# Seven products for the second group's first tile pair, with a raw tile outside the pool, in a two-layer decoder trunk

## The chip, the cores and the metric

The kernel runs on one core of one Trainium2 chip. A core has TensorE (PE in the profile; its weight loads are PEld), VectorE (DVE), ScalarE (ACT), GpSimd (POOL) and SyncE (SP), which here only issues transfers. The metric is the device time of one execution in microseconds, lower is better; the figure shown is the median of several runs.

## The reference, cut to what matters

A trunk of two layers over 512 tokens and 16 meta tokens (L = 528), model width 1024, float32. Each layer is a mixer and an MLP, each followed by a LayerNorm. Both MLPs have the change.

```python
def sq_relu_mlp(h, w1, w2):            # w1: 1024 x 4096, w2: 4096 x 1024
    return jnp.square(jax.nn.relu(h @ w1)) @ w2

for i in range(DEPTH):                 # DEPTH = 2
    mix = retention_gdn_mixer(...) if i % 2 == 0 else mamba2_mixer(...)
    h = layer_norm(DN_ALPHA * h + mix, ln1_w[i], ln1_b[i])
    h = layer_norm(DN_ALPHA * h + sq_relu_mlp(h, mlp_w1[i], mlp_w2[i]), ln2_w[i], ln2_b[i])
return h[:, N_META:]
```

## The kernel before, in words

Activations lie feature-major: a tile has 128 features on the partitions and tokens along the columns. Every float32 operand of a large product is split into a rounded high part and the low rest (`split`, L152 a cast on ScalarE and L153 a subtraction on VectorE), and a product is three matmuls: high by high, high by low, low by high (`mm3`, L172 to L174). Tokens come in two halves: 272 and 256 columns in layer 0, 256 and 256 in layer 1; layer 1 also has the form with 512 columns at once (`both` in `phase`).

**Order.** The Python program writes instructions in an order, with background generators (`tasks`) that `tick()` moves on by a step after each tile. A scheduler at compile time then sets, by its own cost estimates and by that order as priority, the order on each engine; it also waits for buffers. On the chip each engine works through its list in order, and so does SP's queue of transfers.

**Raw weights.** `wtile` takes a tile of 128 x 1024 from the pool "w" of 12. `fetch` (L160) loads a raw tile, `halve` takes two more for its high and low parts, and the raw tile is free when it is split.

**The norm.** `norm_after` spawns a task for each half. It transposes, normalises, transposes back, and for each of 8 tiles m writes the high part on ScalarE (L337), the whole value on VectorE (L339) and the low part `hl` by a subtraction (L340), on VectorE for m = 3 and 7, else on POOL.

**The MLP.** `mlp` goes through the 4096 hidden features in 8 groups of 4 tiles. The first product of a group is either classical, one tile at a time (`phase`), or goes by `Unit`: two tiles at once as a 2 x 2 block product with seven block products of 12 matmuls in place of eight (Winograd's form of Strassen, L510). A unit's `prepare` loads three raw tiles (t1, t2 and x; L472, L473), forms four sums and differences on VectorE (L483 to L487) and splits seven operands; its `run` copies three partial results on ScalarE (L514, L517, L520) and adds them on VectorE (L523, L527, L531). The other factor of the block product are combinations of the norm's output, formed once per MLP by `combos` on VectorE and split (L404, L153), collected in `tt`. Each hidden tile is then passed through ReLU and square (`evac_u`: L447 and L455 on ScalarE, L449 on POOL, L456 on VectorE). `Four` is the second product: four output tiles of one group, accumulated on VectorE (L381 the first time, L379 later).

Before, group 0 is classical: three tiles in the head (first halves of all three, then, when the norm's second half is ready, their second halves), then the fourth. Of group 1, tiles 0 and 2 are classical and 1 and 3 a unit. From there a list of stages runs; during stage i, `adv` moves on the preparation of stage i + 1, and the fetches of stage i + 2 are issued at its start:

```python
        stages = [unit(1, 1), four(0, 0), four(0, 1)]
        for c in range(2, NG):
            stages += [unit(c, 0), four(c - 1, 0), unit(c, 1), four(c - 1, 1)]
```

The last group's second product is done by `Rows` and `final` in layer 1, with the last LayerNorm in it; its weight and bias (`lnf`) lie in the tile that held the tables of layer 0's mixer (`cr`).

Of the kernel before, what the change touches and what calls it, by code (L numbers as in the profile page):

```python
# [57 lines left out]
def trunk(ctx: ExitStack, tc: tile.TileContext, a, out):  # L58
# [7 lines left out]
    def nm(p):  # L66
        count[0] += 1
        return f"{p}{count[0]}"
# [29 lines left out]
    def spawn(gen):  # L98
        tasks.append(gen)
        return gen  # L100
# [18 lines left out]
    def wait(cond):  # L119
        while not cond():  # L120
            yield
# [6 lines left out]
    cst = one("cst", C_COLS)  # L128
    pp = one("pp", PP_COLS)
    rbc = one("rbc", 104)  # L130
    cr = sb.tile([P, R_COLS], F32, tag="cr", bufs=1, name="cr")
    ident = cst[:, C_ID:C_ID + P]
    triu = cst[:, C_TRIU:C_TRIU + P]
    ls = cst[:, C_LS:C_LS + P]
# [19 lines left out]

    def wtile(dt=F32R):
        return sb.tile([P, 1024], dt, tag="w", bufs=12, name=nm("w"))

    def fetch(src, n=1024):
        raw = wtile(F32)
        SY.dma_start(raw[:, :n], src)  # L160
        return raw
# [25 lines left out]
    def phase(tiles, rhs, evac, ns, head=0, tail=0, ready=None):  # L187

        def both(blks, key):
            o = pm(512)
            product(o, blks, rhs[2], every=4)
            for hf in range(2):
                evac(key, hf, o[:, hf * 256:hf * 256 + 256])
            tick()

        def run(hf, blks, key, m=P):
            o = pm(ns[hf], part=m)
            product(o, blks, rhs[hf], m=m)  # L200
            evac(key, hf, o)
            tick()
        n = len(tiles)
        for i0, i1 in [(0, head)] + [(i, i + 1) for i in range(head, n - tail)] + [(n - tail, n)]:
            held = []
            for srcs, *key in tiles[i0:i1]:
                held.append(([b for s in srcs for b in (s if isinstance(s, list) else s() if callable(s) else wload(s))], *key))
                if len(rhs) > 2 and head <= i0 < n - tail:
                    both(*held.pop())
                    continue  # L210
                if ready is not None and i0 == 0:
                    until(lambda: ready(0))
                run(0, *held[-1])
            if ready is not None and i0 == 0:
                until(lambda: ready(1))
            for args in held:
                run(1, *args)
# [91 lines left out]
    def norm_after(r, ns, wcol, bcol):  # L309

        res, pairs = [[], []], []
        if ns[0] + ns[1] == 512:
            res.append([])

        def task(hf):
            n, norm = ns[hf], []

            def apply(off, bn, pt, mean, rstd):
                row = tl("row", 1024)
                t2 = [row[:, j * 512:(j + 1) * 512] for j in range(2)]  # L320
                S.activation(t2[1][:bn], pt[1][:bn, :], AF.Identity, bias=shift(mean, rstd, bn), scale=rstd)
                V.tensor_scalar(t2[0][:bn], pt[0][:bn, :], mean, rstd, op0=SUB, op1=MUL)
                norm.append((off, bn, t2))

            yield from layernorm(r[hf], ns, hf, lambda: hf == 0 or len(res[0]) == KT, apply)
            yield
            for m in range(KT):
                pf = px(n)
                for off, bn, t2 in norm:
                    T.transpose(pf[:, off:off + bn], t2[m // 4][:bn, (m % 4) * P:(m % 4 + 1) * P], ident[:bn, :bn])  # L330
                if hf == 0:
                    pairs.append(htile())
                    if len(res) > 2:
                        res[2] += parts(pairs[m], [(0, 512)])
                hi, lo = parts(pairs[m], [(hf * ns[0], n)])[0]
                w, b = pp[:, wcol + m:wcol + m + 1], pp[:, bcol + m:bcol + m + 1]
                S.activation(hi, pf, AF.Identity, bias=b, scale=w)  # L337
                t = r[hf][m]
                V.tensor_scalar(t, pf, w, b, op0=MUL, op1=ADD)  # L339
                (V if m % 4 == 3 else G).tensor_tensor(lo, t, hi.bitcast(F32), op=SUB)  # L340
                res[hf].append((hi, lo))
        for hf in range(2):
            spawn(task(hf))
        return res, pairs, lambda hf: len(res[hf]) == KT
# [42 lines left out]
    def combos(h, ns, nh, go, get):  # L387

        def quarter(k, c):

            a, b = h[0][k], h[1][k]
            if c == 0:
                return [(0, nh, a[:, 0:nh])]
            cut = ns[0] - nh
            return ([(0, cut, a[:, nh:ns[0]])] if cut else []) + [(cut, nh, b)]

        def diff(out, x, y):
            if not isinstance(y, list):
                y = [(0, nh, y)]
            for o, e, ap in x:  # L400
                for o2, e2, ap2 in y:
                    lo, hi = max(o, o2), min(e, e2)
                    if lo < hi:
                        V.tensor_tensor(out[:, lo:hi], ap[:, lo - o:hi - o], ap2[:, lo - o2:hi - o2], op=SUB)  # L404

        yield from wait(go)
        for k in range(4):
            q0, q1 = [[quarter(i, c) for c in range(2)] for i in (k, k + 4)]
            d = [tl("m", nh) for _ in range(4)]
            diff(d[0], q0[1], q0[0])  # L410
            diff(d[2], q1[1], q0[1])
            diff(d[1], q1[1], d[0])
            diff(d[3], q1[0], d[1])
            for j in range(4):
                get(j, k, d[j])
                if j % 2:
                    yield

    def mlp(l, hx, h, ns, ready, evac0, pairs, final=None):
# [42 lines left out]
        class Unit:  # L462


            def __init__(self, c, i, evac):
                self.src = [w1[l, c * GF + i], w1[l, c * GF + i + 2]]
                self.keys, self.evac, self.ops = (i, i + 2), evac, {}
                self.gen = self.prepare()

            def prepare(self):  # L470
                t1, t2, x = fetch(self.src[0]), wtile(F32), wtile(F32)
                SY.dma_start(x[:, 0:512], self.src[1][:, 0:512])  # L472
                SY.dma_start(t2[:, 512:1024], self.src[1][:, 512:1024])  # L473
                a11, a12, s1, a22, s3, s2 = [y[:, i:i + 512] for y in (t1, t2, x) for i in (0, 512)]
                a21 = s3
                yield

                def sp(x):
                    hi, lo = tl("s", 512, F32R), tl("s", 512, F32R)
                    split(hi, lo, x)  # L480
                    return hi, lo
                s4 = tl("s", 512)
                V.tensor_tensor(s1, a21, a22, op=ADD)  # L483
                V.tensor_tensor(s3, a11, a21, op=SUB)
                yield
                V.tensor_tensor(s2, s1, a11, op=SUB)
                V.tensor_tensor(s4, a12, s2, op=SUB)  # L487
                yield
                self.ops["a11"], self.ops["a12"] = halve(t1)
                yield  # L490
                self.ops["s1"], self.ops["a22"] = halve(t2)
                yield
                self.ops["s2"] = sp(s2)
                yield
                self.ops["s3"] = sp(s3)
                yield
                self.ops["s4"] = sp(s4)
# [88 lines left out]
        def unit(c, i):  # L586
            return Unit(c, i, lambda f, hf, o: groups[c][1](f, hf, o, nh))

        def four(c, i):
            return Four(c, groups[c][0], 4 * i)  # L590

        stages = [unit(1, 1), four(0, 0), four(0, 1)]
        for c in range(2, NG):
            stages += [unit(c, 0), four(c - 1, 0), unit(c, 1), four(c - 1, 1)]
        last = [four(NG - 1, 0), four(NG - 1, 1)] if final is None else [Rows()]
        gens = [st.gen for st in stages + last]
        spawn(combos(h, ns, nh, lambda: ready(1), get))
        phase([([w1[l, f]], f) for f in range(GF)], hx, groups[0][1], ns, head=3, ready=ready)
        spawn(gens[0])
        phase([([w1[l, GF + f]], f) for f in (0, 2)], hx, groups[1][1], ns)  # L600
        until(lambda: "s4" in stages[0].ops and all(x is not None for y in tt for x in y))
        B += [[half(k, 0) for k in range(4)], [half(k, 0) for k in range(4, 8)],
              [half(k, 1) for k in range(4, 8)], tt[3], tt[0], tt[1], tt[2]]
        next(gens[1])
# [389 lines left out]
        put_fm(*done[:3], outs)  # L994
        oF[8 + 2 * hd:10 + 2 * hd] = outs

    dtab, qdec, kdec = cr[:, R_D:R_D + 512], cr[:, R_Q:R_Q + 512], cr[:, R_K:R_K + 8]
    cosT, sinT = cr[:, R_COS:R_COS + L], cr[:, R_SIN:R_SIN + L]

    def rope_tile(block, done):  # L1000
        m1, m2 = tl("s", L), tl("s", L)
# [113 lines left out]
    for hd in range(4):  # L1115
# [1 line left out]
            qF[hd] = f  # L1117
            spawn(gdn_queries(hd))
        conv_tile(a["w0"][4 + hd], gcv[4 + hd], None, done)
    SY.dma_start(cr, a["cstr"])  # L1120
    for hd in range(4):
        got = []
        for i in range(4):
# [35 lines left out]
    h = hn  # L1159


    lnf = sb.tile([P, 2048], F32, tag="cr", bufs=1, name="lnf")
    SY.dma_start(lnf, a["lnf"].unsqueeze(0).to_broadcast([P, 2048]))
    sd = {}

    def ssd_scalars(fm):
# [234 lines left out]
    def final(u, blks, r):  # L1401


        w, b = [lnf[:, j:j + 512] for j in (0, 512)], [lnf[:, j:j + 512] for j in (1024, 1536)]

        def store(t, c0, c1, x, queue=SY):
            queue.dma_start(out[t * P:(t + 1) * P, c0:c1], x)
# [149 lines left out]
```

## Time and profile before

| | |
|---|---|
| time, median of 3 runs | 1700.62 us (1700.37 to 1701.94) |
| time of the profiled execution | 1703.35 us |
| its span, first to last instruction | 1701.6 us |
| granted TensorE clock, mean | 0.991 |
| busy: TensorE, VectorE, ScalarE, POOL | 98%, 68%, 43%, 19% of the span |
| transfers | 155.60 MB, 91 GB/s |

Matmuls overlap each other, so the busy share of TensorE says little; what it really waited for stands in the list of waits, and what a matmul really takes is the distance between two starts. In rows of the order of time, the bracket gives the engine's idle time before the row and what ended it. In the chain of work that ended last, a row is a piece of that chain. In grouped rows stand the count, the busy time in us, the mean in ns, and the idle time before them with what ended it. In rows of stretches of time stand, behind the length, the busy us of PE, PEld, DVE, ACT and POOL with their instructions, then the granted clock of TensorE, the share of the transfer engines and GB/s.

### The profile page before, as it was taken

What the parts mean: (1) busy time and instruction counts of PE and PEld (TensorE: products, weight loads), DVE (VectorE), ACT (ScalarE), POOL (GpSimd) and SP (SyncE); (2) the same over time, 40 slices, a digit from 0 to 9 for tenths busy, and PEclk for the clock granted to TensorE, in tenths of its full rate; (3) what the DMA queues carried; (4) which work ended last, traced back from release to release, by engine and by line L of the source; (5) the groups of instructions that cost most, each with busy time, mean ns of one, the idle gap of its engine ahead of it and who ended that gap; (6) DMA issues with size and microseconds to landing.
All of it is one profiled execution on the core that took longest, in us unless ns stands there. A gap on an engine that the chain in (4) does not pass through costs nothing.

```text
span 1701.6 us, 29956 instructions
## 1 busy us (share of the span) xinstructions
PE 1662.8 (98%) x11884; PEld 1532.8 (90%) x11884; DVE 1152.1 (68%) x2294; ACT 739.7 (43%) x1509; POOL 329.4 (19%) x366
## 2 busy tenths in 40 slices
PE   9999999999999999999999999999999999999998
PEld 7898998899998999999998988888778888888886
DVE  6896666676437766676657776867564686777765
ACT  4432245554214534444434665756432454444441
POOL 1211210010003201111102034232410321111112
PEclk9999999999999999999999999999999999999999
DMA  6233212112221232322221443433222232322321
GB/s 217 81 101 85 72 39 80 45 63 75 87 88 56 94 100 100 100 92 89 94 78 63 127 125 106 118 112 97 84 68 100 74 101 100 100 100 100 100 100 50
DMA packets 88197, 155.60 MB, mean 91 GB/s; under 512 B 11833, under 2 KB 43193, under 8 KB 87801
## 3 DMA queue, kind: packets, MB, share of 16 engines
q1 hardware_dynamic: 87912, 153.53, 28.0%
q8 instruction: 93, 1.52, 0.4%
q14 instruction: 48, 0.39, 0.1%
q10 hardware_dynamic: 144, 0.16, 0.0%
HBM read 148.92 MB, written 4.75 MB: 90 GB/s over the span
## 4 chain that ended last, share of the span: by engine, by line
PE 81%; DVE 7%; DMA 3%; ACT 3%; POOL 3%; issue 2%; SPq 0%; POOLq 0%; DVEq 0%; ACTq 0%
PE pmm L172 18%; PE pmm L174 18%; PE pmm L173 18%; PE pmm L510 8%; PE pmx L510 6%; DVE w L153 1%; PE pmx L1419 1%; DMA w<-in_w 1%; DVE s L633 1%; DMA w<-in_mw 1%; POOL hl L340 1%; PE pmx L1273 1%; DMA row<-rd 1%; PE pmx L1277 1%; PE pmx L270 1%
## 5 line engine op out<-in xcount | busy, mean ns | idle before, releaser
L172 PE MATMUL pmm<-hh,w 128*128 128x256 f32 (+4 forms) x1480 | 456.0, 308 | 4.5 <-ACT s L626 2.6
L173 PE MATMUL pmm<-hl,w 128*128 128x256 f32 (+3 forms) x1480 | 442.3, 299 | 5.5 <-POOL hl L340 4.8
L174 PE MATMUL pmm<-hh,w 128*128 128x256 f32 (+3 forms) x1480 | 443.8, 300 | 0.2 <-DVE w L153 0.2
L152 ACT CAST w<-w 128x1024 fp32r<-128x1024 f32 (+2 forms) x253 | 261.1, 1032 | 410.9 <-PE pmm L174 170.4
L153 DVE TENSOR_TENSOR w<-w,w 128x1024 fp32r<-128x1024 f32 (+2 forms) x253 | 321.3, 1271 | 121.4 <-PE pmm L173 71.5
L172 PE MATMUL pmm<-s,w 128*128 128x256 f32 (+2 forms) x1136 | 361.5, 318 | 0.1
L174 PE MATMUL pmm<-s,w 128*128 128x256 f32 (+2 forms) x1136 | 360.9, 318 | 0.0
L173 PE MATMUL pmm<-s,w 128*128 128x256 f32 (+2 forms) x1136 | 360.4, 317 | 0.0
L172 PEld LDWEIGHTS pmm<-hh,w 128*128 128x128 f32 (+2 forms) x1480 | 279.7, 189 | 18.6 <-issue 4.5
L173 PEld LDWEIGHTS pmm<-hl,w 128*128 128x128 f32 (+1 forms) x1480 | 279.4, 189 | 17.4 <-POOL hl L340 6.1
L174 PEld LDWEIGHTS pmm<-hh,w 128*128 128x128 f32 (+1 forms) x1480 | 279.3, 189 | 8.8 <-DVE w L153 0.7
L174 PEld LDWEIGHTS pmm<-s,w 128*128 128x128 f32 x1136 | 213.8, 188 | 14.6
L172 PEld LDWEIGHTS pmm<-s,w 128*128 128x128 f32 x1136 | 213.9, 188 | 14.4 <-DVE m L381 0.3
L173 PEld LDWEIGHTS pmm<-s,w 128*128 128x128 f32 x1136 | 213.6, 188 | 14.5 <-DVE s L1352 0.3
L449 POOL TENSOR_TENSOR m<-m 128x256 f32<-128x256 f32 (+2 forms) x128 | 120.4, 943 | 512.0 <-ACT m L447 490.2
L147 POOL TENSOR_TENSOR n<-n,neg 128x1 f32<-128x1 f32 (+2 forms) x58 | 40.3, 698 | 440.3 <-DVE n L146 419.7
L633 DVE SCALAR_TENSOR_TENSOR s<-s,pp,s 128x528 f32<-128x528 f32 x120 | 101.7, 848 | 28.1 <-ACT s L631 25.9
L379 DVE TENSOR_TENSOR m<-m,pmm 128x272 f32<-128x272 f32 (+1 forms) x208 | 82.6, 416 | 19.5 <-PE pmm L174 18.8
L456 DVE TENSOR_TENSOR s<-m,s 128x256 fp32r<-128x256 f32 (+2 forms) x128 | 68.2, 535 | 28.5 <-POOL m L449 26.1
L510 PE MATMUL pmm<-s,s 128*128 128x264 f32 (+1 forms) x624 | 85.0, 286 | 2.1 <-ACT row L514 1.8
L510 PEld LDWEIGHTS pmm<-s,s 128*128 128x128 f32 x624 | 79.5, 191 | 2.7 <-ACT row L514 2.0
L1229 POOL TENSOR_TENSOR row<-row,m 128x1024 f32<-128x1024 f32 x16 | 41.0, 2564 | 112.4 <-ACT s L631 57.5
(313 smaller groups left out, 2436.4 us busy)
## 6 DMA issues: line engine op xcount, KB each, us to landing
w<-in_w SPq DMA_DIRECT2D x88, 512.0 KB, 3.3
w<-in_mw SPq DMA_DIRECT2D x172, 256.0 KB, 3.2
w<-in_mw SPq DMA_DIRECT2D x38, 512.0 KB, 3.2
w<-in_wo SPq DMA_DIRECT2D x29, 512.0 KB, 3.5
row<-rd SPq DMA_DIRECT2D x16, 512.0 KB, 5.6
s<-rd SPq DMA_DIRECT2D x32, 128.0 KB, 5.7
w<-in_w2n SPq DMA_DIRECT2D x4, 512.0 KB, 5.6
out<-row SPq DMA_DIRECT2D x7, 256.0 KB, 2.0
```

Of the source, the lines that this page charges most:

```text
L147: G.tensor_tensor(dst, t, neg5[0:part, 0:n], op=POW)
L152: S.copy(dst_hi, src)
L153: V.tensor_tensor(dst_lo, src, dst_hi.bitcast(F32), op=SUB)
L172: T.matmul(o, w[0], x[0], start=first, stop=False)
L173: T.matmul(o, w[0], x[1], start=False, stop=False)
L174: T.matmul(o, w[1], x[0], start=False, stop=last)
L379: V.tensor_tensor(t, t, o, op=ADD)
L449: G.tensor_tensor(q, t, t, op=MUL)
L456: V.tensor_tensor(lo, q, hi.bitcast(F32), op=SUB)
L510: T.matmul(o, w[x][:, c], B[b][k][y], start=first and k == i == 0, stop=last and k == 3 and i == 2, skip_group_check=True)
L633: V.scalar_tensor_tensor(acc, cin[:, k:k + L], w[k], acc, op0=MUL, op1=ADD)
L1229: G.tensor_tensor(g3(rw, 8), g3(rw, 8), bm(cb, 8), op=MUL)
```

## The change

In words: (1) the third raw tile x of a unit no longer comes from the pool of 12 but from one of two tiles, "cra" for a group's first unit and "crb" for its second; these hold layer 0's tables until its mixer is done, loaded by two transfers, and the final norm's weight and bias at the end, now loaded within `final`. (2) In the second half of a norm, VectorE takes the low parts of tiles 3, 5, 6, 7 and POOL those of 0, 1, 2, 4. (3) The raw tile of group 0's fourth tile is fetched behind that of the third, and the fetches of four(0,0) start two ticks after the norm is ready. (4) Group 1's classical pair is gone: unit(1,0) takes its place, and the stages begin with four(0,0), unit(1,0), four(0,1), unit(1,1). (5) `combos` begins one tick later.

```diff
-    cr = sb.tile([P, R_COLS], F32, tag="cr", bufs=1, name="cr")
+    cra, crb = one("cra", R_COS), one("crb", 2 * L)
...
+    def spare(tag):
+
+        return sb.tile([P, 1024], F32, tag=tag, bufs=1, name=nm("sp"))
...
-                (V if m % 4 == 3 else G).tensor_tensor(lo, t, hi.bitcast(F32), op=SUB)
+                (V if m % 4 == 3 or hf == 1 and m > 4 else G).tensor_tensor(lo, t, hi.bitcast(F32), op=SUB)
...
         yield from wait(go)
+        yield
         for k in range(4):
...
-                self.keys, self.evac, self.ops = (i, i + 2), evac, {}
+                self.keys, self.evac, self.ops, self.tag = (i, i + 2), evac, {}, "cr" + "ab"[i]
...
-                t1, t2, x = fetch(self.src[0]), wtile(F32), wtile(F32)
+                t1, t2, x = fetch(self.src[0]), wtile(F32), spare(self.tag)
...
-        stages = [unit(1, 1), four(0, 0), four(0, 1)]
+        def begin():
+            yield from wait(lambda: ready(1))
+            yield from pause(2)
+            yield from gens[0]
+
+        stages = [four(0, 0), unit(1, 0), four(0, 1), unit(1, 1)]
...
         spawn(combos(h, ns, nh, lambda: ready(1), get))
-        phase([([w1[l, f]], f) for f in range(GF)], hx, groups[0][1], ns, head=3, ready=ready)
-        spawn(gens[0])
-        phase([([w1[l, GF + f]], f) for f in (0, 2)], hx, groups[1][1], ns)
-        until(lambda: "s4" in stages[0].ops and all(x is not None for y in tt for x in y))
+        spawn(begin())
+        ahead = []
+
+        def third():
+            blks = wload(w1[l, 2])
+            ahead.append(fetch(w1[l, 3]))
+            return blks
+
+        phase([([w1[l, 0]], 0), ([w1[l, 1]], 1), ([third], 2), ([lambda: halve(ahead[0])], 3)], hx, groups[0][1], ns,
+              head=3, ready=ready)
+
+        until(lambda: len(stages[0].blks) == 4 and all(x is not None for y in tt for x in y))
...
-    dtab, qdec, kdec = cr[:, R_D:R_D + 512], cr[:, R_Q:R_Q + 512], cr[:, R_K:R_K + 8]
-    cosT, sinT = cr[:, R_COS:R_COS + L], cr[:, R_SIN:R_SIN + L]
+    dtab, qdec, kdec = cra[:, R_D:R_D + 512], cra[:, R_Q:R_Q + 512], cra[:, R_K:R_K + 8]
+    cosT, sinT = crb[:, 0:L], crb[:, L:2 * L]
...
-    SY.dma_start(cr, a["cstr"])
+    SY.dma_start(cra, a["cstr"][:, 0:R_COS])
+    SY.dma_start(crb, a["cstr"][:, R_COS:R_COLS])
...
-    lnf = sb.tile([P, 2048], F32, tag="cr", bufs=1, name="lnf")
-    SY.dma_start(lnf, a["lnf"].unsqueeze(0).to_broadcast([P, 2048]))
...
-        w, b = [lnf[:, j:j + 512] for j in (0, 512)], [lnf[:, j:j + 512] for j in (1024, 1536)]
+        w, b = [], []
+        for i, (dst, tag) in enumerate(((w, "cra"), (b, "crb"))):
+            x = spare(tag)
+            SY.dma_start(x, a["lnf"][i * 1024:(i + 1) * 1024].unsqueeze(0).to_broadcast([P, 1024]))
+            dst += [x[:, 0:512], x[:, 512:1024]]
```

## The prediction

> **What bounds the kernel now.** I read the page first, then who waited for whom, then the order of time around the start of each MLP, then the grouped instructions of VectorE (DVE) there.
>
> ```profile
> span 1701.6 us, 29956 instructions
> PE 1662.8 (98%) x11884; PEld 1532.8 (90%) x11884; DVE 1152.1 (68%) x2294; ACT 739.7 (43%) x1509; POOL 329.4 (19%) x366
> PE 81%; DVE 7%; DMA 3%; ACT 3%; POOL 3%; issue 2%; SPq 0%; POOLq 0%; DVEq 0%; ACTq 0%
> ```
>
> TensorE is the bound: 81% of the chain. So time can be won in two ways only: fewer matmuls, or less waiting between them. The rows below are matmuls in order of time (start, duration, line, and in brackets the idle time and its releaser), at the start of MLP 0 and then of MLP 1.
>
> ```profile
> 545.78 0.28 PE L172 MATMUL pmm<-hh,w 128*128 128x256 f32 x1
> 550.87 0.58 PE L173 MATMUL pmm<-hl,w 128*128 128x256 f32 x1 [2.39 <-POOL hl L340]
> 551.24 0.42 PE L174 MATMUL pmm<-hh,w 128*128 128x256 f32 x1
> 551.46 0.42 PE L172 MATMUL pmm<-hh,w 128*128 128x256 f32 x1
> 558.71 0.29 PE L172 MATMUL pmm<-hh,w 128*128 128x272 f32 x1
> 564.58 0.29 PE L172 MATMUL pmm<-hh,w 128*128 128x272 f32 x1
> 576.33 0.28 PE L510 MATMUL pmm<-hh,w 128*128 128x264 f32 x1
> 581.22 2.83 PE L510 MATMUL pmm<-s,s 128*128 128x264 f32 x12 [1.80 <-ACT row L514]
> 590.17 0.28 PE L172 MATMUL pmm<-s,w 128*128 128x272 f32 x1
> ...
> 1351.41 0.29 PE L172 MATMUL pmm<-hh,w 128*128 128x256 f32 x1
> 1356.48 0.58 PE L173 MATMUL pmm<-hl,w 128*128 128x256 f32 x1 [2.38 <-POOL hl L340]
> 1364.29 0.40 PE L172 MATMUL pmm<-hh,w 128*128 128x512 f32 x1
> 1380.94 0.28 PE L510 MATMUL pmm<-hh,w 128*128 128x256 f32 x1
> 1391.80 0.40 PE L172 MATMUL pmm<-s,w 128*128 128x512 f32 x1
> ```
>
> Next, the undisturbed price of a stage, from the chain (start, duration, twelve matmuls of one product): in MLP 0 the first and last product of one unit, the first of the next and the first of the last unit; then first and last product of a unit of MLP 1.
>
> ```profile
> 614.14 1.46 PE pmm L510 x12
> 622.92 1.46 PE pmm L510 x12
> 636.09 1.45 PE pmm L510 x12
> ...
> 857.34 1.46 PE pmm L510 x12
> 1435.42 1.43 PE pmm L510 x12
> 1443.97 1.43 PE pmm L510 x12
> ```
>
> A unit takes 622.92 + 1.46 - 614.14 = 10.24 us in MLP 0, a Four 636.09 - 624.38 = 11.71; in MLP 1 a unit takes 1443.97 + 1.43 - 1435.42 = 9.98. A matmul of 256 columns costs 1.43/12 = 0.119.
>
> With these prices the losses stand out. The second halves of the first three tiles are 72 matmuls of 256 columns, 8.6 us; they take 558.71 - 545.78 = 12.9 and 1364.29 - 1351.41 = 12.9. So 4.3 us go in each MLP: 2.4 of waiting for POOL, and the rest because the matmuls behind it start 0.22 apart (551.24, 551.46), half rate. The first unit takes 590.17 - 576.33 = 13.84 instead of 10.24 (3.6 lost) and 1391.80 - 1380.94 = 10.86 instead of 9.98 (0.9 lost).
>
> **The change part by part.**
>
> *Norm shares.* In the second half the subtractions of tiles 5 and 6 go from POOL to DVE. POOL's last one in MLP 0, and DVE's rows of this stage:
>
> ```profile
> 547.76 3.06 POOL L340 TENSOR_TENSOR hl<-m,hh 128x256 fp32r<-128x256 f32 x1
> 543.46 2.35 DVE L339 TENSOR_SCALAR m<-pmx,pp 128x256 f32<-128x256 f32 x5
> 546.42 1.44 DVE L339 TENSOR_SCALAR m<-pmx,pp 128x256 f32<-128x256 f32 x3
> L340 DVE TENSOR_TENSOR hl<-m,hh x4: 411/672/812, 530.3 to 548.1; 128x272 fp32r<-128x272 f32 x2, 128x256 fp32r<-128x256 f32 x2
> ```
>
> The op that held TensorE is POOL's sixth, 3.06 us to 550.82. Its fifth ended where the sixth begins, at 547.76, so without the last two POOL is done before that. DVE's L339 end at 547.8; three subtractions at 0.41, each starting about 0.08 before its predecessor is done, give tiles 5, 6, 7 at 548.15, 548.5, 548.85. TensorE asks for them at 545.78 + 16 x 0.119 = 547.7, then 0.36 apart. So some 0.5 us of waiting is left, now on DVE, and the gain is 4.3 - 0.5 = 3.8 per MLP, 7.6 in all. Layer 0's last norm gets the same edit; no wait of its matmuls on POOL's hl stands in the list of waits there, so I cost it at nothing; if DVE is late there, it is tenths.
>
> *The pair becomes a unit.* Two classical tiles of group 1: 576.33 - 564.58 = 11.75 in MLP 0; in MLP 1 two of the three tiles in 1380.94 - 1364.29, 11.1. A unit: 10.24 and 9.98. Gain 1.5 + 1.1 = 2.6.
>
> *The order and the fetches.* four(0,0) now stands where the pair stood, so the first unit still has one stage of 11 to 12 us in front of it. Its loss of 3.6 came from late weights:
>
> ```profile
> SPq L549 <- PE pmm L174: 11.8, 1, 11.8
> 579.85 1.04 ACT L152 CAST w<-w 128x1024 fp32r<-128x1024 f32 x1 [1.04 <-DMA w<-in_mw]
> 552.54 0.38 SPq L160 DMA_DIRECT2D w<-in_mw  x1
> 574.55 3.19 SPq L549 DMA_DIRECT2D w<-in_mw  x6
> ```
>
> SP issues in order; after 552.54 it came to a Four's loads and stood 11.8 us until a tile of the pool of 12 was free, so that most of them went out at 574.55. The cast at 579.85 waited for it on ScalarE, with the copy L514 that TensorE needed queued behind. After the change the unit's third raw tile is outside the pool: a Four's four halves, the next unit's two raws and four halves and the next Four's two raws make exactly 12, where they made 13. The third fetch is one issue earlier, the Four's four loads start two ticks after the norm, and nothing waits in SP ahead of them. I take both losses as gone: 3.6 + 0.9 = 4.5.
>
> *Steady stretch.* From 614.14 to 857.34 are 11 steps of a unit and a Four: 243.2 against 11 x 21.95 = 241.4, 1.8 lost; DVE's first sum of a unit (L483) waits for the raw tiles, 27 us in 11 times:
>
> ```profile
> DVE w L483 <- DMA w<-in_mw: 27.0, 11, 3.8
> ```
>
> I take 1.5 of the 1.8 (ends 0 and 1.8). MLP 1 runs at 21.1 and gives nothing.
>
> *What it adds: DVE.* This is the term against the change. The pair's two splits and four evacuations are replaced by a Four's two splits and eight evacuations, then a full unit. DVE in MLP 0 from 543.4 to 576.3, grouped (count, busy, mean ns, idle before), and the engines' busy time in the two stretches of it:
>
> ```profile
> L153 DVE TENSOR_TENSOR s<-m,s 128x264 fp32r<-128x264 f32 x16 | 6.9, 448 | 0.0
> L153 DVE TENSOR_TENSOR w<-w,w 128x1024 fp32r<-128x1024 f32 x4 | 5.2, 1328 | 2.0 <-ACT w L152 2.0
> L404 DVE TENSOR_TENSOR m<-m,m 128x256 f32<-128x256 f32 x12 | 4.9, 412 | 0.0
> L456 DVE TENSOR_TENSOR s<-m,s 128x256 fp32r<-128x256 f32 x5 | 3.3, 668 | 1.0 <-POOL m L449 1.0
> 546.00:558.70 12.70, 10.30 (x72) 9.89 (x71) 9.53 (x25) 5.71 (x16) 6.15 (x7) 0.87 0.17 63
> 558.70:570.45 11.75, 11.75 (x98) 11.75 (x97) 10.73 (x31) 7.64 (x22) 4.83 (x6) 1.00 0.14 46
> ```
>
> With 0.08 off each duration for the overlap, until the unit's first operand: combinations 16 x 0.37, their differences 16 x 0.33 and some narrow ones, 11.6; norm 8 x 0.46 and four subtractions, 5.2; seven L456, 3.9; four splits at 1.25, 5.0; four sums and differences of 512 columns at 0.6, half a 1024 wide split with its overlap off, 2.4; eight evacuations like a 256 wide difference, 2.7. That is 30.8 from 543.46, hence 574.3 without a gap. TensorE arrives at 545.78 + 8.6 + 0.5 + 5.87 + 11.7 = 572.4. DVE is 1.9 late with no idle time, 6.1 with the 4.2 us of idle it showed here (2.0 + 1.0, and 1.2 of the other L456 group). Part of that idle was the late fetch: I take 4. MLP 1 has no narrow pieces (nine fewer instructions) and its first unit lost only 0.9 against 3.6, so I take half, 2, with the ends 0 and 4. In the same places lies the other new wait: four(0,0) reads group 0's last tile at once, whose square must pass ScalarE, POOL and DVE; the two are one queue on DVE, so I count them once. I expect these 6 us in pieces under a microsecond (three PSUM buffers pace the Four), hence without the half rate.
>
> Trainium skill, "TensorE: Matmul & The Clock Gate", section "What's actually happening": the clock falls to half only after an idle window of about 3.4 us. By that rule the stall of 2.39 would have cost 2.4 and not 4.3; this trace's 0.22 us steps right behind it say otherwise, so the sum stays with the rows.
>
> *lnf, the split of cr, the extra yield.* The final norm's weights were loaded long ahead and are now two loads behind the last fetches, into tiles free since the last units' splits; their first reader is the first final row, at least a Four stage later. The two cr loads carry the same bytes at the start of the run. The yield delays the combinations by one tick, behind the norm's subtractions. Nothing each.
>
> **Sum.** 7.6 + 2.6 + 4.5 + 1.5 = 16.2 gained, 6 given back: 10.2. The profiled execution took 1703.35 us (1701.6 and 1.75 around it), 2.7 above the median; 1693.1 on its scale is 1690.4 on the median's.
>
> **The rivals.**
>
> *A, no backlog:* the order of DVE's work lets the first operands pass the combinations. For it: only 9.53 of 12.70 us of DVE busy. Against it: 10.73 of 11.75 right after. 1684.4.
>
> *B, port instead of engine:* the moved subtractions meet POOL's squares. At 0.8 each, the long end of DVE's own row (812), they end at 547.8 + 2.4 = 550.2, 1.8 late instead of 0.5, and a wait of 1.8 is followed by half rate, as at 581.22 (2.83 for twelve): 1.3 and 1.9 per MLP more, 1696.8. Against it: without its last two POOL is done before DVE begins. Trainium skill, "SBUF — State Buffer", section "SBUF: two separate sides": DVE with two SBUF inputs and POOL hold the port by turns, the other blocking; the 3.06 us op agrees.
>
> *C, DVE becomes the bound, and it is slower:* unit(2,0) follows unit(1,1) with no Four between. Until its first operand DVE has 30.8 + 3.05 + 2.5 + 2.5 + 2.7 + 6.7 + 2.5 + 3.65 = 54.4 us (rest of the unit's operands, its evacuation, Four, next unit, and so on). At the 75% of the first stretch that is 72.5, to 616.0; TensorE would be there at 572.4 + 10.2 + 11.7 + 10.2 = 604.5: 11.5 lost, and in MLP 1, with nine small instructions fewer, some 11. 16.2 - 22.5 = -6.3: 1706.9. It decides from about 79% of useful DVE time downwards. Against it: 91% in the second stretch, and the idle partly came from the late fetch.
>
> *D, it moves nothing:* backlog of 13 to 16 eats it, 1697.4 to 1700.6.
>
> **How the numbers follow.** Main case, gain 7 to 14 (1686.6 to 1693.6), 50%; A 17%; B 13%; D 11%; C 9%. Within 0.2% (3.4 us, about what a measurement can tell from no change) is D. Faster 0.80, same 0.11, slower 0.09. Range: up to the best A with all of 1.8 and no residual wait (1683) and to D's end, 1700.
>
> **What would show it.** Right: no wait on POOL hl L340 at either MLP start, clock there near 1.00 instead of 0.87; no SP wait of 11.8; L483 waiting little for DMA; 12 matmuls fewer in MLP 0 and 36 more, shorter ones, in MLP 1. Wrong: waits of L172 or L510 on DVE (L381, L456, L153) at four(0,0), unit(1,0) or unit(2,0), above 3 us per place.

## The result, and the profile after

The change makes the kernel slower: 1714.78 us, median of six runs (1712.83 to 1716.37), against 1700.49 for the kernel before in the same comparison (1695.86 to 1702.44). The ratio is 1.0085, 95% interval 1.0072 to 1.0099. The forecast was 1690.4, in a range of 1683 to 1700. The two profiled executions differ by 13.0 us in span, and the working below goes by these.

The page of the changed kernel first: span, busy time, and the shares of the chain of work that ended last.

```profile
span 1714.6 us, 29979 instructions
PE 1661.8 (97%) x11908; PEld 1530.1 (89%) x11908; DVE 1163.5 (68%) x2320; ACT 745.9 (44%) x1521; POOL 315.4 (18%) x360
PE 78%; DVE 8%; issue 4%; POOL 4%; ACT 3%; DMA 3%; SPq 0%; POOLq 0%; DVEq 0%; ACTq 0%
```

VectorE is at 68%, as before: no engine has become the bound. But TensorE's share of the chain fell from 81% to 78%. The list of waits says for what (engine, line, what it waited for: us in total, times, longest). First one row of the kernel before, then the changed kernel:

```profile
PE pmm L510 <- DVE row L527: 1.0, 2, 0.5
```

```profile
PE pmm L515 <- DVE row L532: 14.1, 27, 0.9
PE pmm L177 <- DVE s L461: 2.5, 2, 1.3
PE pmm L176 <- ACT s L460: 2.0, 2, 1.2
```

L532 is the sum x2 + ba of a unit, L527 of before. A wait that came twice in the whole run now comes in 27 of the 28 units. The waits of 4.8 on POOL's hl are gone but for 0.3; two on group 0's last tile (L460, L461) have come.

The first matmul of a unit shows where the time went. Rows in order of time of the changed kernel, unit(2,1) and unit(7,1) of MLP 0, then of MLP 1:

```profile
634.31 0.28 PE L515 MATMUL pmm<-hh,w 128*128 128x264 f32 x1
861.46 0.28 PE L515 MATMUL pmm<-hh,w 128*128 128x264 f32 x1
1440.90 0.28 PE L515 MATMUL pmm<-hh,w 128*128 128x256 f32 x1
1659.08 0.28 PE L515 MATMUL pmm<-hh,w 128*128 128x256 f32 x1
```

A unit and a Four take (861.46 - 634.31)/10 = 22.72 us in MLP 0, against 243.2/11 = 22.11 before, and (1659.08 - 1440.90)/10 = 21.82 in MLP 1 against 21.1 (the values of before stand in the prediction). So eleven such steps lose 6.7 and 7.9 us: 14.6, more than the whole difference. All the rest of the change together gained about 1.6, where the prediction had gains of 14.7 against losses of 6.

Why a unit is late, the chain of work that ended last shows for unit(2,0) (start, duration, what):

```profile
617.47 0.60 ACT w L152
618.07 0.35 issue
618.42 0.43 ACT m L452
618.91 1.35 POOL m L454
620.29 0.43 DVE s L461
620.73 0.35 DVE row L532
621.12 1.73 PE pmm L515 x12
```

In the chain of the kernel before a unit is seven rows of PE and nothing else. Here the chain leaves TensorE after the fourth product (a12) and goes through a cast of weights, the ReLU and the square of a hidden tile, and two instructions of VectorE, until the last product (a22), which adds into the PSUM tile that L532 reads, can start: 1.73 for its twelve instead of 1.46, and a gap ahead of it. The cast itself isn't new: in the kernel before it starts at the same place in the unit (620.04, which is 6.1 us after the unit's first matmul, here 5.9). What is new stands on VectorE.

VectorE's own list in the next unit, unit(2,1), in order of time, in the kernel before and in the changed one. L523, L527, L531 are the sums x1 + bb, x2 + ba, x3 + bc before, L528, L532, L536 the same after; L456 and L461 are the evacuations; L153 with 1024 columns is the split of the next unit's first raw tile.

```profile
642.01 0.43 DVE L523 TENSOR_TENSOR row<-row,pmx 128x264 f32<-128x264 f32 x1 [2.23 <-PE pmx L510]
643.47 0.43 DVE L527 TENSOR_TENSOR row<-row,pmm 128x264 f32<-128x264 f32 x1 [1.03 <-PE pmm L510]
...
647.05 1.65 DVE L153 TENSOR_TENSOR w<-w,w 128x1024 fp32r<-128x1024 f32 x1
```

```profile
640.45 0.43 DVE L528 TENSOR_TENSOR row<-row,pmx 128x264 f32<-128x264 f32 x1 [4.45 <-PE pmx L515]
641.34 1.22 DVE L153 TENSOR_TENSOR w<-w,w 128x1024 fp32r<-128x1024 f32 x1 [0.47 <-ACT w L152]
643.09 0.43 DVE L461 TENSOR_TENSOR s<-m,s 128x264 fp32r<-128x264 f32 x1 [0.52 <-POOL m L454]
643.44 0.42 DVE L532 TENSOR_TENSOR row<-row,pmm 128x264 f32<-128x264 f32 x1
```

Before, both sums come first, and the split starts 3.6 us after the second. After, the split and one evacuation stand between the sums, and the second ends 3.0 us after the first instead of 1.5. The evacuation waits for POOL's square, which takes longer beside the split. POOL's row in the changed kernel, then in the kernel before:

```profile
641.71 1.35 POOL L454 TENSOR_TENSOR m<-m 128x264 f32<-128x264 f32 x1 [17.39 <-ACT m L452]
```

```profile
643.40 0.63 POOL L449 TENSOR_TENSOR m<-m 128x264 f32<-128x264 f32 x1 [16.11 <-ACT m L447]
```

The square started at 641.71 and the split ran until 642.56; from there the square needs 0.50. Trainium skill, "SBUF — State Buffer", section "SBUF: two separate sides": an instruction of VectorE with two inputs in SBUF and one of GpSimd that reads SBUF share a port, and the one that starts first holds it for its whole length, the other one blocked. The trace agrees: 1.35 beside the split, 0.63 without it.

So the theory, called T: with x outside the pool of 12 a pool tile is free earlier, the split of the next unit's first tile can be placed earlier, and at compile time it is put ahead of x2 + ba. VectorE has the time for it (it stood idle 4.45 us just before), but TensorE's last product is behind it.

The start of the MLP has the second loss. MLP 0 by stretches (length; busy us of PE, PEld, DVE, ACT, POOL; granted clock, DMA share, GB/s): norm and group 0, the start of four(0,0).

```profile
545.00:557.60 12.60, 12.52 (x103) 12.32 (x103) 12.06 (x32) 6.78 (x19) 5.23 (x7) 1.00 0.40 127
557.60:570.50 12.90, 10.41 (x63) 9.98 (x62) 11.33 (x33) 6.95 (x18) 3.46 (x4) 0.75 0.06 20
```

And rows in order of time there, of TensorE, then of ScalarE and VectorE:

```profile
562.97 0.51 PE L176 MATMUL pmm<-s,w 128*128 128x272 f32 x2 [1.20 <-ACT s L460]
564.77 0.59 PE L177 MATMUL pmm<-s,w 128*128 128x272 f32 x1 [1.29 <-DVE s L461]
561.75 0.41 ACT L152 CAST s<-m 128x264 fp32r<-128x264 f32 x1 [0.75 <-DVE m L408]
562.07 0.39 ACT L452 ACTIVATE m<-pmm 128x272 f32<-128x272 f32 x1
568.62 0.75 DVE L385 SCALAR_TENSOR_TENSOR m<-m,pmm 128x272 f32<-128x272 f32 x2
```

The norm's wait and its half rate are gone (clock 1.00 up to 557.60). But four(0,0) waits 1.20 and 1.29 for the square of group 0's last tile, and then runs at half rate until 570.7: 5.7 us lost, of which 2.8 in these two gaps from start to start and about as much in some 28 matmuls that start 0.1 late each. (This second half hangs on where the waits fall, as the last section shows: in e5 below the same two waits have no half rate behind them.) That tile's product had been finished for about 4 us when ScalarE came to its ReLU at 562.07: casts of the combinations stood ahead, and waited for VectorE (L408). In MLP 1 the same two waits are 0.84 and 1.22 with no half rate behind them, 2.6 lost.

### The profile page after: what moved, and what is told of

Its sections match the earlier page's. It is cut to its first block, busy times and chain, and to the rows that moved or that the text cites. A ratio compares the mean times of both kernels' runs of the same rounds, so it can differ in the third digit from the quotient of the medians.

```text
span 1714.6 us, 29979 instructions
## 1 busy us (share of the span) xinstructions
PE 1661.8 (97%) x11908; PEld 1530.1 (89%) x11908; DVE 1163.5 (68%) x2320; ACT 745.9 (44%) x1521; POOL 315.4 (18%) x360
## 4 chain that ended last, share of the span: by engine, by line
PE 78%; DVE 8%; issue 4%; POOL 4%; ACT 3%; DMA 3%; SPq 0%; POOLq 0%; DVEq 0%; ACTq 0%
PE pmm L178 18%; PE pmm L177 18%; PE pmm L176 18%; PE pmm L515 7%; PE pmx L515 4%; POOL m L454 3%; DMA w<-in_w 2%; DVE s L651 1%; ACT w L152 1%; PE pmx L1440 1%; DVE w L153 1%; DVE s L461 1%; PE pmx L334 1%; PE pmx L274 1%; PE pmx L1290 1%
## 5 line engine op out<-in xcount | busy, mean ns | idle before, releaser
L176 PE MATMUL pmm<-hh,w 128*128 128x256 f32 (+6 forms) x1432 | 437.7, 306 | 6.4 <-ACT s L644 4.5
L178 PE MATMUL pmm<-hh,w 128*128 128x256 f32 (+6 forms) x1432 | 427.0, 299 | 0.6 <-DVE w L153 0.6
L177 PE MATMUL pmm<-hl,w 128*128 128x256 f32 (+6 forms) x1432 | 425.0, 297 | 1.0 <-DVE hl L153 0.5
L153 DVE TENSOR_TENSOR w<-w,w 128x1024 fp32r<-128x1024 f32 (+2 forms) x253 | 312.2, 1235 | 144.5 <-PE pmm L177 77.9
L176 PEld LDWEIGHTS pmm<-hh,w 128*128 128x128 f32 (+2 forms) x1432 | 268.7, 188 | 19.5 <-ACT s L644 5.0
L177 PEld LDWEIGHTS pmm<-hl,w 128*128 128x128 f32 (+2 forms) x1432 | 268.8, 188 | 10.9 <-issue 2.1
L178 PEld LDWEIGHTS pmm<-hh,w 128*128 128x128 f32 (+2 forms) x1432 | 269.0, 188 | 8.1 <-DVE w L153 0.9
L454 POOL TENSOR_TENSOR m<-m 128x256 f32<-128x256 f32 (+2 forms) x128 | 113.9, 891 | 536.7 <-ACT m L452 516.7
L461 DVE TENSOR_TENSOR s<-m,s 128x256 fp32r<-128x256 f32 (+2 forms) x128 | 64.0, 503 | 42.1 <-POOL m L454 41.2
L515 PE MATMUL pmm<-s,s 128*128 128x264 f32 (+1 forms) x672 | 89.8, 283 | 0.0
L515 PEld LDWEIGHTS pmm<-s,s 128*128 128x128 f32 x672 | 84.5, 188 | 0.0
L528 DVE TENSOR_TENSOR row<-row,pmx 128x264 f32<-128x264 f32 (+1 forms) x28 | 11.9, 425 | 92.3 <-PE pmx L515 92.3
```

What stands on the lines that cost most here:

```text
L153: V.tensor_tensor(dst_lo, src, dst_hi.bitcast(F32), op=SUB)
L176: T.matmul(o, w[0], x[0], start=first, stop=False)
L177: T.matmul(o, w[0], x[1], start=False, stop=False)
L178: T.matmul(o, w[1], x[0], start=False, stop=last)
L454: G.tensor_tensor(q, t, t, op=MUL)
L461: V.tensor_tensor(lo, q, hi.bitcast(F32), op=SUB)
```

## The experiments

Times are medians, each with its ratio to the runs of the kernel before on the same chip (their median between 1699.9 and 1701.9).

**Parts undone and done alone.** Four kernels: the change without the third tile's own place, the kernel before with nothing but that place (and the two table tiles and the late load of the last norm's weights that go with it), the kernel before with nothing but the norm's shares, and the change with the unit's two sums put together.

```diff
 e1: changed kernel
-                t1, t2, x = fetch(self.src[0]), wtile(F32), spare(self.tag)
+                t1, t2, x = fetch(self.src[0]), wtile(F32), wtile(F32)
 e2: kernel before
-                t1, t2, x = fetch(self.src[0]), wtile(F32), wtile(F32)
+                t1, t2, x = fetch(self.src[0]), wtile(F32), spare(self.tag)
 e3: kernel before
-                (V if m % 4 == 3 else G).tensor_tensor(lo, t, hi.bitcast(F32), op=SUB)
+                (V if m % 4 == 3 or hf == 1 and m > 4 else G).tensor_tensor(lo, t, hi.bitcast(F32), op=SUB)
 e4: changed kernel
                 V.tensor_tensor(x1, x1, bb, op=ADD)
-                evac(keys[0], 0, x1)
-                adv()
                 prod(ba, "s3", 6, False, False)
                 V.tensor_tensor(x2, x2, ba, op=ADD)
+                evac(keys[0], 0, x1)
+                adv()
                 evac(keys[1], 1, x2)
```

The change without x's own place (unit starts and lengths are read from the trace of each run, a unit from first to last matmul start):

> The changed kernel with one word put back: the unit's third raw tile x comes from the pool of 12 again. Theory T (order on VectorE): with x outside the pool a pool tile is free one step earlier, so VectorE splits the next unit's first raw tile (1.22 us) between a unit's first and second addition and takes a square's low part ahead of the second addition; the last product, which goes into the same PSUM tile, waits 0.6 us and a unit takes 11.0 us instead of 10.1. With x back the second addition comes first again in 20 of 28 units, so most units take 10.1 to 10.3 us; 1714.8 - 20 x 0.9 and 1 to 4 us of late fetches at the MLP starts: 1699 (1695 to 1704). Rival S (the new order of stages, a unit behind a unit, leaves VectorE behind for good): units stay at 11.0, 1714 or more.

Measured 1699.78, ratio 0.9997 (0.9981 to 1.0014): the loss is gone. VectorE's order in 20 of the 28 units is the old one. The rest of the change, so, is worth nothing here: VectorE's waits for raw tiles are back (row below), and unit(2,0) takes 11.9.

```profile
DVE w L488 <- DMA w<-in_mw: 48.3, 21, 3.8
```

The place alone:

> The kernel before, with nothing but the third raw tile outside the pool (and the two table tiles and the late load of the last norm's weights that go with it); classical pair, norm and order of stages as before. T: units at 11.0 us, 24 or 25 of 26, so 1700.5 + 24 x 0.9 and up to 2 us back for earlier fetches: 1720 (1717 to 1723). S: units at 10.1, 1699 to 1701.

Measured 1713.47, ratio 1.0082 (1.0064 to 1.0101), the whole loss from this one edit. Its list of waits has the same wait (L530 is its x2 + ba), and on VectorE the split and one evacuation stand between the two sums in all 26 units:

```profile
PE pmm L513 <- DVE row L530: 13.1, 26, 0.6
```

The expected 1720 was too high, because this edit keeps the gains of fewer fetch waits too: unit(1,1) of MLP 0 takes 11.0 instead of 13.7.

The norm's shares alone:

> The kernel before, with nothing but the norm's even shares. T and S alike: no wait on POOL for the low parts at the MLP starts, 3.8 us less in each, 1693 (1691 to 1695). Rival N (the wait is taken over by what comes next, the fetches for the pair and the unit): the first unit waits longer, 1697 to 1701.

Measured 1696.82, ratio 0.9984 (0.9973 to 0.9995): by the ratio 2.7 us, about a third of what was expected. TensorE's and VectorE's rows there say why:

```profile
549.61 0.38 PE L173 MATMUL pmm<-hl,w 128*128 128x256 f32 x1 [0.48 <-DVE hl L340]
551.01 0.39 PE L172 MATMUL pmm<-hh,w 128*128 128x256 f32 x1 [0.91 <-ACT m L447]
548.80 0.41 DVE L404 TENSOR_TENSOR m<-m,m 128x256 f32<-128x256 f32 x1
549.14 0.41 DVE L340 TENSOR_TENSOR hl<-m,hh 128x256 fp32r<-128x256 f32 x1
```

A combination (L404) stands on VectorE ahead of tile 7's subtraction (L340), and its cast on ScalarE ahead of the ReLU that frees a PSUM tile. In the changed kernel neither wait is there; the one extra tick, which starts the combinations later, is tried alone below.

The two sums together:

> The changed kernel with one line moved: a unit's first result is passed on (ReLU, square) only behind its second addition, so that the addition stands ahead of the square's low part on VectorE; the split of 1.22 us stays between the two additions. T: units back to 10.1 to 10.2, 1714.8 - 27 x 0.9 = 1691 (1688 to 1695). Rival P (the split itself holds VectorE too long there, whatever the order behind it): units at 10.7 or more, 1708 to 1715. S: 11.0, 1714.

Measured 1695.06, ratio 0.9979 (0.9964 to 0.9994). The split still stands ahead of x2 + ba, but the evacuation does not, and that is enough:

```profile
638.82 0.43 DVE L528 TENSOR_TENSOR row<-row,pmx 128x264 f32<-128x264 f32 x1 [4.45 <-PE pmx L515]
639.72 1.23 DVE L153 TENSOR_TENSOR w<-w,w 128x1024 fp32r<-128x1024 f32 x1 [0.47 <-ACT w L152]
640.86 0.42 DVE L530 TENSOR_TENSOR row<-row,pmm 128x264 f32<-128x264 f32 x1
```

The second sum (L530 here) ends 2.0 after the first, and a unit and a Four take 21.93 and 21.10. The split by itself is hidden, then. So is the evacuation by itself: in the run with x in the pool, unit(1,0) and unit(1,1) of MLP 0 have the evacuation without the split between the two sums (at 584.07 and 606.07, its square 0.63 on POOL), the second sum ends 2.0 after the first, and they take 10.12 and 10.13, as an undisturbed unit does. So it is split and evacuation together, with the latter's path through ScalarE and the slowed POOL, that make TensorE late.

**Is it the free tile, or the place? And the wait at four(0,0).** Three more on the changed kernel: another cure for the order (the product s3 ahead of a12), a pool of 11 in place of 12, and, with e4's edit, a first Four that does three hidden tiles for three outputs before any output asks for the last one.

```diff
 e5: prod(ba, "s3", ...), its sum and evacuation ahead of prod(bb, "a12", ...) and its own
 e6: e4, and in the run of stages[0]
+                    for j, hf in jobs[:3]:
+                        o = outs[j, hf] = pm(512 if wide else ns[hf])
+                        product(o, [self.blks[j]], self.u[hf], k1=3)
+                    ...  # then k = 3 of these, then the other outputs
 e7: changed kernel
-        return sb.tile([P, 1024], dt, tag="w", bufs=12, name=nm("w"))
+        return sb.tile([P, 1024], dt, tag="w", bufs=11, name=nm("w"))
```

> The changed kernel with 11 tiles in the weights' pool in place of 12, the third raw tile still outside it; raw tiles and halves together are as many as before the change. Theory T (the tile that came free in the pool lets the next unit's split be put ahead of x2 + ba): VectorE's order in the unit is again both sums before the split, units 10.1 and 9.83 us, 1700 (1695 to 1706, by the waits for fetches that come back). Rival X (the place of x itself does it, by its own tile's release or its loads): units stay at 11.0 and 10.8, 1713 to 1717.

Measured 1700.01, ratio 0.9998 (0.9985 to 1.001), with x still in its own place. The two sums follow each other again, the evacuation behind them:

```profile
643.63 0.43 DVE L528 TENSOR_TENSOR row<-row,pmx 128x264 f32<-128x264 f32 x1 [2.32 <-PE pmx L515]
645.09 0.43 DVE L532 TENSOR_TENSOR row<-row,pmm 128x264 f32<-128x264 f32 x1 [1.03 <-PE pmm L515]
645.67 0.43 DVE L461 TENSOR_TENSOR s<-m,s 128x264 fp32r<-128x264 f32 x1 [0.15 <-POOL m L454]
```

Theory T holds: it is the free tile. The place itself costs nothing that these times show.

> The changed kernel with the unit's products a12 and s3 in the other order, so that the sum x2 + ba comes first on VectorE and the split of the next unit's first raw tile can only fall behind both sums. Theory T (the unit is late because that split and one evacuation stand ahead of x2 + ba): units go back to 10.1 and 9.83 us, time 1695 (1692 to 1699), like the kernel that puts the two sums together. Rival U (the split costs TensorE its time wherever it lies in the unit, by ScalarE's cast or by POOL's square beside it): units above 10.5, 1703 to 1711.

Measured 1701.23, ratio 1.0005 (0.9991 to 1.002): outside what either theory expected. The units take 10.36 and 10.1. The order on VectorE is cured (both sums ahead of the split in 27 of 28 units), but a new 0.27 comes at another place: s2 and s3 now follow each other into one PSUM tile, and by the program s3 must wait for ScalarE's copy between them. The row of s3 in the chain, unit(2,1); a product takes 1.46 there otherwise:

```profile
637.01 1.73 PE pmm L515 x12
```

28 times 0.24 is 6.7; it stays behind e4 by 4.4 us by the ratios and by 6.2 by the medians. The product a12 had covered that copy.

> The changed kernel with the two sums together, and in the first four(0,0) of an MLP the first three outputs do hidden tiles 0 to 2 before any of them asks for tile 3, which group 0 has only just finished. Theory W (TensorE waits there for that tile's square, 1.4 + 1.5 us and 2.8 of half rate behind it in MLP 0, 0.9 + 1.5 in MLP 1): both waits go, 7 less than with the sums alone, 1688 (1685 to 1690). Rival B (VectorE's backlog is behind it and comes out a stage later, as the prediction put it): the wait moves to the end of four(0,0) or to unit(1,0), 1693 to 1695.

Measured 1697.08, ratio 0.9978 (0.9963 to 0.9994), no better than e4, and slower than either expectation; the mechanism is rival B's. TensorE gets 27 matmuls further and then stands longer, for a free PSUM tile:

```profile
568.59 0.38 PE L176 MATMUL pmm<-s,w 128*128 128x256 f32 x1 [3.04 <-DVE m L385]
```

L385, the Four's first addition, starts at 568.1 on VectorE, as it did in the changed kernel (568.62): it stands behind the combinations. So the late square is one face of a queue.

**The queue at four(0,0).** Two kernels with e4's edit: one without combinations, whose units read plain tiles of the norm's output in their place, so that it computes something else, and one that holds three of their four groups back until four(0,0) has begun and completes them before unit(1,0).

```diff
 f2
-        spawn(combos(h, ns, nh, lambda: ready(1), get))
-        until(lambda: len(stages[0].blks) == 4 and all(x is not None for y in tt for x in y))
+        until(lambda: len(stages[0].blks) == 4)
+        for j in range(4):
+            for k in range(4):
+                tt[j][k] = half(k + 4 * (j % 2), j // 2)
 f3
+            if k == 1:
+                yield from wait(late)          # late: stages[0] has begun
-        until(lambda: len(stages[0].blks) == 4 and all(x is not None for y in tt for x in y))
+        until(lambda: len(stages[0].blks) == 4)
...
+            if i == 0:
+                until(lambda: all(x is not None for y in tt for x in y))
```

> The changed kernel with the two sums together, and without the combinations: they are neither formed nor split, and the units of both MLPs read plain tiles of the norm's output in their place. It leaves out 16 sums and 16 splits of 264 or 256 columns per MLP. Theory Q (what TensorE waits for at four(0,0) is the queue of ScalarE and VectorE, in which the last tile's ReLU and square and the first additions of the Four stand behind the combinations): the waits and the half rate there go, 5.7 + 2.6 less than the 1695 with the sums alone, 1687 (1684 to 1690). Rival W (the path of the square itself, ScalarE to POOL to VectorE, is too long for a reader that comes at once): at least half of the waits stay, 1691 to 1695.

Measured 1690.01, ratio 0.9929 (0.9913 to 0.9946). By the ratios that is 0.5%, 8.5 us, less than e4 (some 5 to 12 by the two intervals). What is left of the waits in MLP 0 is 0.55 and 0.70, with no half rate:

```profile
565.34 0.39 PE L176 MATMUL pmm<-s,w 128*128 128x256 f32 x1 [0.55 <-ACT s L460]
566.42 0.39 PE L177 MATMUL pmm<-s,w 128*128 128x256 f32 x1 [0.70 <-DVE s L461]
```

> The changed kernel with the two sums together, and with three of the four groups of combinations held back until four(0,0) begins, all of them done before unit(1,0). Theory Q: the last tile's square and the Four's first additions pass them, TensorE gets through four(0,0) without a wait of over 1 us, and what is left of the queue comes out at unit(1,0), in MLP 0 at most 2 to 3 us: 1691 (1688 to 1694). Rival R (VectorE simply has too much work before unit(1,0), so its order moves nothing): what four(0,0) gains unit(1,0) loses, 1694 to 1698.

Measured 1693.82, ratio 0.9956 (0.9939 to 0.9972), 0.23% or 3.9 us less than e4. One wait of 0.54 is left at four(0,0) of MLP 0; part comes back in MLP 1, where unit(1,1) waits 1.40 for its sum x2 + ba and unit(2,0) 1.03 for an operand that is split late:

```profile
1402.47 1.69 PE L517 MATMUL pmm<-s,w 128*128 128x256 f32 x12 [1.40 <-DVE row L532]
1408.16 1.45 PE L517 MATMUL pmm<-s,s 128*128 128x256 f32 x10 [1.03 <-DVE s L153]
```

**The tick, and a share of the queue.** The kernel before with the norm's shares and the one extra tick, and f3 with two groups held back (`if k == 2`) in place of three.

> The kernel before with the norm's new shares and the one extra tick ahead of the combinations, nothing else of the change. In the run of the shares alone the first combination stood on VectorE ahead of tile 7's subtraction, and TensorE waited 0.5 for that and 0.9 for ScalarE behind it in each MLP. Theory Y (the tick is what keeps the combinations behind the norm): both waits go, 3 us less than with the shares alone, 1693 (1691 to 1695), ratio to before 0.996. Rival N (the tick only moves the combinations' queue to the next stage): as the shares alone, 1696 to 1698, ratio 0.998.

Measured 1694.37, ratio 0.996 (0.9945 to 0.9974), the number of theory Y. Tile 7's subtraction now stands ahead of the combinations, and no wait is left there:

```profile
548.52 0.41 DVE L340 TENSOR_TENSOR hl<-m,hh 128x256 fp32r<-128x256 f32 x1
548.86 0.15 DVE L404 TENSOR_TENSOR m<-m 128x8 f32<-128x8 f32 x1
```

But rival N has a part in it. The first unit takes 13.85 us in MLP 0 and 12.80 in MLP 1, where it took 11.55 and 11.25 with the shares alone; in MLP 0 half rate follows its wait of 1.94. From the first matmul of the MLP to the start of unit(2,1), the profiled executions took 97.8 and 93.7 with the shares alone and 98.0 and 92.3 with the tick. By the two ratios the tick is worth 4 us, by their intervals 1 to 7; so its size stays open.

> As the kernel that holds three of the four groups of combinations back until four(0,0) begins, but only the last two groups are held. Theory Q (a queue of fixed length that is only shared out between four(0,0) and unit(1,0)): the wait at four(0,0) comes back in part and unit(1,0) gains the same, 1693 to 1695, as with three groups. Rival: the half rate makes the place count, with fewer held back the waits fall under what sets it off in both places, 1690 to 1692.

Measured 1692.51, ratio 0.9942 (0.9923 to 0.996), at the border of the two expectations. The waits at four(0,0) are 1.06 and 0.90 in MLP 0 and one of 2.03 in MLP 1, with no half rate behind them, and the units behind lose less than with three groups. Its interval overlaps that of three groups, so which of the two is better stays open. It is the fastest full computation here: every part of the change kept, with two edits of order, 0.6% below the kernel before, 1.4% below the changed one by the ratios.

## Why the prediction was wrong, point by point

- **Steady stretch: the step that failed.** The prediction gave the freed tile a gain of 1.5, for fewer waits for raw tiles. These waits did fall, from 51.1 us in 23 in the whole run to 8.4 in 6:

```profile
DVE w L488 <- DMA w<-in_mw: 8.4, 6, 3.2
```

  But the stretch was bound by TensorE, which an earlier split can't help, and the split took a place ahead of a sum that TensorE waits for: 6.7 and 7.9 lost, where -1.5 and 0 stood. e2 (all of the loss by this edit alone), e1 and e7 (none without the free tile) and e4 (gone with the order mended) show it. The prediction asked what moves earlier on the queues of transfers; it did not ask it of VectorE's list, which is put in order anew when a buffer comes free earlier. Its signs of being wrong were waits above 3 us at three places; this loss came in 27 waits, none above 0.9, and the one at four(0,0) in waits of at most 1.29.
- **Norm shares: right in kind; right in size only with the tick, which was put at nothing.** Its 7.6 answers to 1701.72 x 0.004 = 6.8 (4.4 to 9.4 by the interval) in g1, shares and tick together. The shares alone gave 0.16%, 2.7 us (0.9 to 4.6). What the prediction left out of its reckoning of tiles 5 to 7 stood in the trace of the kernel before: a combination (L404) at 547.78, ahead of tile 7's subtraction at 548.11.
- **First unit and fetches: right, but in part hidden by the late sums.** unit(1,1), the first unit before, takes 11.07 us in MLP 0 from first to last matmul start instead of 13.72, and 10.37 in e4, where the order is mended. In MLP 1 it takes 11.07 instead of 10.74, and 10.02 in e4. So some 3.3 of the 3.6 and 0.7 of the 0.9 were there to be had. unit(1,0) takes 10.12 in MLP 0 where the pair took 11.75, so the 1.5 came too; in MLP 1 unit(1,0) is late like all others (10.83).
- **Backlog: near in size, wrong in kind.** Forecast 4 and 2, "in pieces under a microsecond, hence without the half rate", reckoned at the first operand of unit(1,0). Measured 5.7 and 2.6, all a stage earlier at four(0,0), in two waits each, with half rate behind them in MLP 0, some 2.8 of the 5.7. f2 shows that the combinations are the source: 8.5 (5 to 12) for the 8.3. f2 takes their work away as well as their place; f3 and g2, which move only the place, get 3.9 and 6.3 us of it by the ratios. So what stood first in VectorE's list and in ScalarE's was a good part of it.
- **Rival C** had the right sign for the wrong reason: unit(2,0) of MLP 0 came at 611.5, 2.4 us earlier than before, so VectorE kept up. **A** and **B** priced the same places; neither had a mechanism for the order inside a unit.
- **Not foreseen, small:** the first product of the state-space mixer waits 3.9 instead of 2.0 for its input (L644). It is there in e4 too (4.5). What brings it was not tried.

## What to carry to other kernels

When a scheduler sets the order, a freed buffer is not only a wait less: everything that may now start earlier can be put ahead of something else. List for the engine in between which instruction of the bound engine's next step could fall behind it, and where two results are needed by the bound engine, write them next to each other in the program, with the evacuations behind. Before moving work to a place that reads a fresh result at once, look at the in-order lists that this result passes, not at the busy shares of their engines.

## What the runs showed of the hardware

The half rate depends on where waits fall, and not only on their length. In the changed kernel, waits of 1.20 and 1.29 us that ended 1.8 apart (562.97 and 564.77) set it off: the granted clock is 0.50 from 564.09 to 570.92. In e5 the same two waits, 1.19 and 1.29, ended 1.8 apart too (563.39 and 565.19), and the clock stayed at 1.00. In e4, waits of 0.70 and 1.22 in MLP 1 set it off at 1369.37.

In each trace the stretches of half rate start whole multiples of 3.41 us apart (in the changed kernel 564.09, 915.66 and 980.52: 103 and 122 of them behind the first). Cut on that grid, these are the stretches with the waits: one of the changed kernel, two of e5, one of e4.

```profile
560.68:564.09 3.41, 1.60 (x11) 1.17 (x9) 2.87 (x9) 2.60 (x8) 1.55 (x2) 1.00 0.00 0
560.11:563.52 3.41, 2.22 (x19) 2.00 (x18) 3.41 (x13) 1.74 (x5) 0.57 (x1) 1.00 0.00 0
563.52:566.94 3.42, 2.13 (x16) 1.92 (x17) 2.89 (x10) 1.46 (x5) 1.31 (x2) 1.00 0.00 0
1365.95:1369.37 3.42, 1.63 (x6) 0.76 (x5) 2.92 (x8) 1.72 (x5) 2.18 (x2) 1.00 0.00 0
```

Where TensorE was busy for 1.60 and 1.63 of a stretch, half rate followed. In e5 the edge fell between the two waits, each of the two stretches was busy for over 2.1, and it did not. What share sets it off stays open: ahead of 915.66 in the changed kernel the stretch was busy for 2.50.

Trainium skill, "TensorE: Matmul & The Clock Gate", section "What's actually happening": the activity is watched in a window of about 3.4 us that runs freely. The grid and the effect of position agree with that. The same section has the clock fall after an idle window; if that means a window without work, these rows don't agree, as TensorE worked for 1.60 of the 3.41 us.
